# State-space input tables built in matmul layout from a repeated power table, in a hybrid S5 and Fourier inference step

## The chip, the cores and the metric

The kernel runs on one core of a Trainium2 chip. The metric is device time in microseconds (us) for one execution of the whole program; less is better. Engines are named as in the profile: PE (matmul), PEld (its weight load), DVE (vector), ACT (scalar), POOL (GpSimd) and SP, which only issues transfers.

## The reference, cut to what matters

One layer is applied to 1024 latent and 128 context tokens: a normalisation with modulation, a projection `z = h @ w_in`, a state-space branch and a Fourier branch, each gated by a sigmoid, an output projection, and a SwiGLU block. The change lies in the projection's gates and in the state-space branch, which per direction computes

```
step = exp(log_step);  a = exp(lam * step)            # complex, one per group and state
f    = (a - 1) / lam                                  # complex
bu   = u @ (f * b).T                                  # 32 groups, 16 inputs, 64 states
s_t  = a * s_(t-1) + bu_t                             # forward and backward
y    = Re(s @ c.T) + d * u
g_s5, g_f = sigmoid(h @ w_gates)                      # 2 x 1024 columns
```

## The kernel before

The tokens are cut into 144 chunks of T = 8 steps (16 context chunks, 128 latent chunks). The 32 groups are handled in NB = 8 steps of GQ = 4 groups. The 128 partitions of a state tile are 2 directions times 64 states. For one step q the kernel needs three tables:

- `W` [128, 2, 4*128], which takes the state at a chunk's start to its 8 outputs. It is built on DVE from the power table `Aw` and the parameters `Cp` (lines 545 to 550, with `Gt` as scratch).
- `Gt`, the input table: for each group a 128 by 128 matrix from (time in chunk, input) to (direction, state), once real and once imaginary. Its entries are `fA[p, t, g] * b[p, g, h]` as complex numbers, where `fA` is the table of `f * a^t`. DVE builds it with the state on the partitions (lines 552 to 561), PE then transposes each 128 by 128 block (line 566, 8 blocks a step), and ACT copies the result back (line 567), so that it can be a matmul's weights.
- `Tm`, the direct path inside a chunk, built by small matmuls (line 594), stored to DRAM as `kd` and loaded back through a sliding window (line 605).

`fA` and `Aw` are copied by DVE from tables that POOL computes (lines 498 to 501), with the time axis reversed for the backward half.

`s5_run(q)` loads the inputs `U` from DRAM, multiplies them by `Gt` (tile `v`, line 621) and copies the result from PSUM to the state tile `X`: the forward half by ACT (line 625), the backward half with the chunk axis reversed by ACT and DVE (lines 627 to 630). DVE then scans `X` over the chunks (lines 636 to 639). `s5_out(q)` copies `X` to `Xo` on ACT (656 to 658), multiplies by `Tm` and `W` (tile `y`, lines 666 to 668) and stores the outputs.

Between these steps stand nine calls `gate(p)`. Each runs two column blocks of the projection through `in_unit`: the weights `ws` are loaded by SP, split into two parts by ACT (line 93) and DVE (line 94), and 72 matmuls a block (lines 271 to 273) fill three PSUM tiles. The first of them carries two more columns, the shift; DVE copies these to `sh` (line 482), and ACT applies the function with `sh` as bias (lines 483 to 486). The finished pieces `sg` are stored to DRAM as `ind`, issued by SP (line 685).

The program order is

```
pre, run_ = [prep(0)], []
gate(ORD[0])
pre.append(prep(1)); run_.append(s5_run(0, ...))
for q in range(NB):
    run_.append(s5_run(q + 1, ...)); gate(ORD[q]); s5_out(q, ...); pre.append(prep(q + 2))
```

This order is only a priority. A planner orders the instructions of each engine by a simulated timeline, and takes what is ready at its simulated time in this priority; the order on each engine is then fixed, and an engine whose next instruction is not ready waits, with all that stands behind it. Waits between engines are semaphores that the framework sets. Tiles of one tag share `bufs` buffers, and a new tile waits for the readers of the one whose buffer it takes.

Of the kernel before, what the change touches and what calls it, by code (L numbers as in the profile page):

```python
# [22 lines left out]
CH = 384  # L23
# [6 lines left out]
T = 8  # L30
# [31 lines left out]
def tile_flow_step(ctx: ExitStack, tc: tile.TileContext, a, o):  # L62
# [17 lines left out]
    def aux_tile(name):  # L80
        return psp.tile([128, 512], F32, tag="aux", bufs=3, name=name)
# [281 lines left out]
    def st(name, shape, bufs=None):  # L363
        return pS.tile(shape, F32, tag=name, name=name, bufs=bufs)
# [110 lines left out]
    def in_unit(j0, nm, piece, out, func):  # L475
        for f in range(2):
            w = weight(a["w_in"][j0 + f], f"{nm}{f}", eng=V)
            sh = psh.tile([128, 2], F32, tag="sh", bufs=2, name=f"sh{f}_{nm}")
            for t in (2, 0, 1):
                ps, dst = proj_unit(w, t, f"{nm}{f}_{t}"), piece(f, t)  # L480
                if t == 2:
                    V.tensor_copy(sh, ps[:, CH:CH + 2])
                    S.activation(out=dst[:, 0:256], in_=ps[:, 0:256], func=func, bias=sh[:, 0:1])
                    S.activation(out=dst[:, 256:CH], in_=ps[:, 256:CH], func=func, bias=sh[:, 1:2])
                else:
                    S.activation(out=dst, in_=ps[:, 0:CH], func=func, bias=sh[:, 0:1])
                out(f, t, dst)
# [8 lines left out]
    u_unit(1, 1)  # L496
    u_unit(2, 1)
    with tc.issue_after(last[1]):
        for e_, d_, s_ in ((V, fA, Fk), (V, Aw, Ak[:, :, 1:9])):
            e_.tensor_copy(d_[0:64], s_[0:64])  # L500
            e_.tensor_copy(d_[64:128], s_[64:128, :, ::-1])
    pSt.release()
    pwa.release()
    abc = open_pool("abc")
    h_chunk(2)
    u_unit(3, 1)
    u_unit(2, 2)
# [10 lines left out]
    pw.release()  # L518
    pwu.release()
    pa.release()  # L520
    psh = open_pool("psh")
    q5 = open_pool("q5", side="right")

    def s5_prep(q):
        gs = slice(GQ * q, GQ * q + GQ)
        Bp = q5.tile([128, 2, GQ, H], F32, tag="Bp", name=f"Bp{q}")
        SY.dma_start(out=Bp, in_=a["b_p"][:, :, gs, :])
        Cp = q5.tile([128, 2, GQ, H], F32, tag="Cp", name=f"Cp{q}")
        SY.dma_start(out=Cp, in_=a["c_p"][:, :, gs, :])
# [12 lines left out]
        W = q5.tile([128, 2, GQ * 128], F32, tag="W", bufs=NW, name=f"W{q}")
        Gt = q5.tile([128, 2, GQ * 128], F32, tag="G", bufs=NG, name=f"G{q}")
        e_ = V
        V.tensor_tensor(v4(W, 0), bt(Aw, 0), bp(Cp, 0), ALU.mult)
        V.tensor_tensor(v4(Gt, 0), bt(Aw, 1), bp(Cp, 1), ALU.mult)
        V.tensor_tensor(W[:, 0], W[:, 0], Gt[:, 0], ALU.add)
        e_.tensor_tensor(v4(W, 1), bt(Aw, 0), bp(Cp, 1), ALU.mult)
        e_.tensor_tensor(v4(Gt, 1), bt(Aw, 1), bp(Cp, 0), ALU.mult)
        e_.tensor_tensor(W[:, 1], W[:, 1], Gt[:, 1], ALU.subtract)  # L550

        V.tensor_tensor(v4(Gt, 0), bt(fA, 0), bp(Bp, 0), ALU.mult)
        V.tensor_tensor(v4(Gt, 1), bt(fA, 1), bp(Bp, 1), ALU.mult)
        V.tensor_tensor(Gt[:, 0], Gt[:, 0], Gt[:, 1], ALU.subtract)
        V.tensor_tensor(v4(Gt, 1), bt(fA, 0), bp(Bp, 1), ALU.mult)
        gh = GQ // 2
        for hh in range(2):
            gt = q5.tile([128, gh, T, H], F32, tag="gt", name=f"gt{q}{hh}")
            hs, gl = slice(128 * gh * hh, 128 * gh * hh + 128 * gh), slice(gh * hh, gh * hh + gh)
            V.tensor_tensor(gt, bt(fA, 1)[:, gl], bp(Bp, 0)[:, gl], ALU.mult)  # L560
            V.tensor_tensor(Gt[:, 1, hs], Gt[:, 1, hs], gt.rearrange("p g t h -> p (g t h)"), ALU.add)

        for ri in range(2):
            ps = aux_tile(f"gtr{q}_{ri}")
            for g in range(4):
                PE.transpose(ps[:, 128 * g:128 * g + 128], Gt[:, ri, 128 * g:128 * g + 128], ident)
            S.copy(out=Gt[:, ri, :], in_=ps)

        return gs, Bp, Cp, W, Gt

    def s5_prep2(q, gs, Bp, Cp, W, Win):
        bb = q5.tile([128, 3, 2, GQ * H + H], F32, tag="bb", name=f"bb{q}")
        b4 = bb[:, :, :, 0:GQ * H].rearrange("p v r (g h) -> p v r g h", g=GQ)
        bt1 = q5.tile([128, 240], F32, tag="KX", name=f"bt1{q}")[:, 0:2 * GQ * H].rearrange("p (r g h) -> p r g h", r=2, g=GQ)
        shb = [128, GQ, H]
        V.memset(bb, 0.0)
        for ri in range(2):
            fb = [fr2[:, r, gs].unsqueeze(2).to_broadcast(shb) for r in range(2)]
            V.tensor_tensor(b4[:, 0, ri], Bp[:, ri], fb[0], ALU.mult)
            V.tensor_tensor(bt1[:, ri], Bp[:, 1 - ri], fb[1], ALU.mult)  # L580
            V.tensor_tensor(b4[:, 0, ri], b4[:, 0, ri], bt1[:, ri],
                            ALU.subtract if ri == 0 else ALU.add)
        V.tensor_copy(bb[0:64, 1], bb[0:64, 0])
        V.tensor_copy(bb[64:128, 2], bb[64:128, 0])
        KX = q5.tile([128, GQ // 4, 240], F32, tag="KX", name=f"KX{q}")
        for aa in range(GQ // 4):
            ps = aux_tile(f"kx{q}_{aa}")
            for v, cs_ in ((2, slice(0, 112)), (0, slice(112, 128)), (1, slice(128, 240))):
                for ri in range(2):
                    for g4 in range(4):  # L590
                        g = 4 * aa + g4
                        src = (Cp[:, ri, g], W[:, ri, 128 * g:128 * g + 112],
                               W[:, ri, 128 * g + 16:128 * g + 128])[v]
                        PE.matmul(ps[32 * g4:32 * g4 + 32, cs_], bb[:, v, ri, H * g:H * g + 32], src,
                                  start=(ri == 0), stop=(ri == 1), skip_group_check=True)
# [10 lines left out]
        return W, Win, Tm  # L606

    def s5_run(q, Win):
        gs = slice(GQ * q, GQ * q + GQ)
# [5 lines left out]
        n = 0  # L615
        for ri in range(2):
            for g0 in range(0, GQ, 2):
                ng = 2
# [4 lines left out]
                v = ps[:, 0:CC * ng].rearrange("p (g c) -> p g c", g=ng)  # L623
                xg = X[:, ri, g0:g0 + ng]
                S.copy(out=xg[0:64, :, 1:CC + 1], in_=v[0:64])
                if n % 2:
                    V.tensor_copy(xg[64:128, :, CP + 1:CC + 1], v[64:128, :, CC - 1:CP - 1:-1])
                else:
                    S.copy(out=xg[64:128, :, CP + 1:CC + 1], in_=v[64:128, :, CC - 1:CP - 1:-1])
                V.tensor_copy(xg[64:128, :, 1:CP + 1], v[64:128, :, CP - 1::-1])  # L630
                n += 1
        def step(lv, dst, src):
            m = dst.shape[3]
            shp = [128, 2, GQ, m]
# [42 lines left out]
    def gate(p):  # L677
# [1042 lines left out]
def _layout(i):  # L1720
# [72 lines left out]
```

## Time and profile before

| | |
|---|---|
| runs of the kernel before | 1524.16 us median of 3 (1522.48 to 1524.55) |
| the profiled execution's own time | 1526.42 us |
| its span, first to last instruction | 1524.6 us |
| mean granted clock of PE in it | 0.981 |
| PE / DVE / ACT / POOL busy | 1460.6 / 946.5 / 567.1 / 662.1 us |
| moved by DMA | 243.84 MB |

The profiled execution's time lies 1.82 us above its span and 2.26 us above the median of the runs. Times in the trace are counted from the start of the span. The state-space steps and the gates take the stretch from about 98 to 400 us.

### The profile page before, as it was taken

Reading aid. Unit: us, or ns where it says so; the run is one execution under the profiler, and the core shown is the slowest. Engines: PE = TensorE matmul, PEld = TensorE weight load, DVE = VectorE, ACT = ScalarE, POOL = GpSimd, SP = SyncE. Lnnn points to the kernel's source line nnn. Section 1 sums busy time; section 2 is a strip of 40 time slices with the busy share of each in tenths; the row PEclk is TensorE's granted clock in tenths of the full one; section 3 lists DMA queues with packets and bytes.
Section 4 is the critical chain, followed back from the end, with each engine's and each line's share of the span. In section 5 each row is a group of like instructions: output and inputs, shape, how many; then the busy total and the mean of one; then the engine's idle time right before and its main releaser. Section 6 shows DMA issues by size and latency. Waiting matters only on the chain. (4 is left out here: it accounts for less than half of the span.)

```text
span 1524.6 us, 23986 instructions
## 1 busy us (share of the span) xinstructions
PE 1460.6 (96%) x8999; PEld 1312.5 (86%) x8999; DVE 946.5 (62%) x1845; ACT 567.1 (37%) x1096; POOL 662.1 (43%) x599
## 2 busy tenths in 40 slices
PE   6999999999989999999899999999999999999995
PEld 3799998989968779787679999999999998887884
DVE  5557989997245335368964345553345567667788
ACT  7433243343444122355543433433333444112323
POOL 4910000000014111354687778877777972322354
PEclk9999999999989999999999999999999999999998
DMA  9343233232524753354431355444445458667523
GB/s 326 106 126 97 75 109 94 89 106 94 176 76 128 247 169 121 128 206 181 170 127 71 111 197 198 158 177 170 171 183 205 188 194 311 215 219 293 192 69 124
DMA packets 101984, 243.84 MB, mean 160 GB/s; under 512 B 15710, under 2 KB 46047, under 8 KB 101868
## 3 DMA queue, kind: packets, MB, share of 16 engines
q1 hardware_dynamic: 93228, 210.84, 40.0%
q10 hardware_dynamic: 8640, 31.46, 5.2%
q8 instruction: 71, 1.16, 0.3%
q14 instruction: 45, 0.37, 0.1%
HBM read 172.51 MB, written 69.74 MB: 159 GB/s over the span
## 5 line engine op out<-in xcount | busy, mean ns | idle before, releaser
L94 POOL TENSOR_TENSOR wh_glu<-ws_glu,wh_glu 128x512 fp32r<-128x512 f32 x4 | 5.1, 1276 | 338.2 <-DMA St<-in_fS 324.0
L271 PE MATMUL g<-h,wh_g 128*128 128x384 f32 (+1 forms) x432 | 147.5, 341 | 0.0
L272 PE MATMUL g<-h,wh_g 128*128 128x384 f32 (+1 forms) x432 | 147.3, 341 | 0.0
L273 PE MATMUL g<-h,wh_g 128*128 128x384 f32 (+1 forms) x432 | 146.5, 339 | 0.0
L1308 DVE TENSOR_TENSOR stg<-ra,stg 128x512 fp32r<-128x512 f32 x63 | 69.5, 1113 | 71.3 <-ACT stg L1307 71.3
L1416 POOL TENSOR_TENSOR wd<-wd,wd 128x512 f32<-128x512 f32 x25 | 36.5, 1474 | 111.7 <-DMA wd<-in_w_d 48.6
L272 PEld LDWEIGHTS g<-h,wh_g 128*128 128x128 f32 x432 | 81.5, 189 | 0.2 <-issue 0.2
L271 PEld LDWEIGHTS g<-h,wh_g 128*128 128x128 f32 x432 | 81.3, 188 | 0.3 <-issue 0.3
L273 PEld LDWEIGHTS g<-h,wh_g 128*128 128x128 f32 x432 | 81.3, 188 | 0.2 <-issue 0.2
L94 POOL TENSOR_TENSOR wh_pj<-ws_pj,wh_pj 128x512 fp32r<-128x512 f32 x16 | 22.1, 1380 | 104.3 <-ACT wh_pj L93 93.0
L1469 DVE TENSOR_TENSOR acc<-acc,U 128x1024 f32<-128x1024 f32 x34 | 41.4, 1219 | 25.3 <-PE U L1450 25.0
L1307 ACT CAST stg<-ra 128x512 fp32r<-128x512 f32 x63 | 38.5, 617 | 36.4 <-DVE ra L1296 28.4
L963 DVE TENSOR_TENSOR wh_out<-ws_out,wh_out 128x512 fp32r<-128x512 f32 x32 | 34.1, 1081 | 23.5 <-ACT wh_out L962 23.5
L1296 DVE TENSOR_TENSOR ra<-ra 128x512 f32<-128x512 f32 x36 | 46.5, 1292 | 0.3
L1450 PE MATMUL q<-B,A 128*128 128x512 f32 x192 | 45.4, 393 | 0.2 <-DVE tq L1599 0.2
L1450 PEld LDWEIGHTS q<-B,A 128*128 128x128 f32 x192 | 36.0, 188 | 8.8 <-DVE tq L1599 0.6
L923 DVE TENSOR_TENSOR sgc<-sgc,p 128x384 f32<-128x384 f32 x24 | 13.3, 554 | 48.4 <-PE p L106 48.4
L963 POOL TENSOR_TENSOR wh_out<-ws_out,wh_out 128x512 fp32r<-128x512 f32 x16 | 22.0, 1380 | 46.5 <-ACT wh_out L962 44.5
L977 PE MATMUL o<-wh_out,m 128*128 128x512 f32 x96 | 37.1, 414 | 3.5 <-ACT scr0b L1059 3.5
L636 DVE TENSOR_TENSOR ta<-X,Sg 128x56 f32<-128x56 f32 (+10 forms) x88 | 39.0, 443 | 1.1
L639 DVE TENSOR_TENSOR X<-X,tb 128x56 f32<-128x56 f32 (+10 forms) x88 | 39.0, 450 | 0.9
L962 ACT CAST wh_out<-ws_out 128x512 fp32r<-128x512 f32 x48 | 28.2, 616 | 29.2 <-PE o L979 18.9
(1550 smaller groups left out, 4516.8 us busy)
## 6 DMA issues: line engine op xcount, KB each, us to landing
ad<-stg ACTq DMA_DIRECT2D x60, 512.0 KB, 2.9
A<-ad SPq DMA_DIRECT2D x60, 512.0 KB, 6.2
wa<-in_w_ada SPq DMA_DIRECT2D x48, 512.0 KB, 6.1
ws_out<-in_w_out SPq DMA_DIRECT2D x24, 512.0 KB, 3.9
wd<-in_w_d SPq DMA_DIRECT2D x22, 512.0 KB, 9.4
ind<-in SPq DMA_DIRECT2D x54, 192.0 KB, 1.9
ws_g<-in_w_in SPq DMA_DIRECT2D x18, 512.0 KB, 3.5
sgc<-ind SPq DMA_DIRECT2D x48, 192.0 KB, 3.3
```

What stands on the lines that cost most here:

```text
L271: PE.matmul(ps, w[:, 0, wsl], hi, start=first, stop=False)
L272: PE.matmul(ps, w[:, 0, wsl], lo, start=False, stop=False)
L273: PE.matmul(ps, w[:, 1, wsl], hi, start=False, stop=last)
L636: V.tensor_tensor(A, src, Sc[:, 0, lv, gs].unsqueeze(1).unsqueeze(3).to_broadcast(shp), ALU.mult)
L639: V.tensor_tensor(dst, dst, B[:, ::-1], ALU.add)
L963: (eng or PL).tensor_tensor(w[:, 1, :], src, f32(w[:, 0, :]), ALU.subtract)
L977: PE.matmul(p, mc[t][0][:, k, ts_], w[n][:, 0], start=(k == 0), stop=False)
L1296: V.tensor_tensor(a_[out], a_[x], a_[y], op)
L1307: S.copy(out=st_[:, 0], in_=src)
L1308: V.tensor_tensor(st_[:, 1], src, f32(st_[:, 0]), ALU.subtract)
L1450: PE.matmul(ps, A[:, va], B[:, vb], start=(first and ti == 0 and i == 0), stop=(last and ti == n - 1 and i == 2), skip_group_check=True)
L1469: V.tensor_tensor(dst, dst, ps, ALU.add)
```

## The change

`Gt` is no longer built with the state on the partitions and transposed. Instead `fA` itself is transposed once, in four 128 by 128 blocks, written to a DRAM table `fad` as three parts (real, minus imaginary, imaginary), and in each step a load repeats each row of that table over 16 partitions (`FA_`), so that it lies as (time, input) on the partitions and (group, state) in the free axis. The parameters `b` come in a second layout `b_t`, made on the host, and a load repeats them over the 8 times (`Bt`). Three DVE operations of 128 by 1024 elements then give `Gt` as the matmul wants it. They stand at the end of `s5_prep2`. The scratch for `W` becomes a tile of its own, `Wt`.

The loads of a step (`Bp`, `Cp`, `FA_`, `Bt`) are issued at the start of the step before, in two buffers each. The stores of the gates' pieces are issued by ACT in place of SP. The copy of the shift columns and the copies of the backward half of the state go from DVE to ACT.

```diff
-    fA = st("fA", [128, 2, T, G])
+    fA = st("fA", [128, 2, NB, T, GQ])
...
-                    V.tensor_copy(sh, ps[:, CH:CH + 2])
+                    S.copy(out=sh, in_=ps[:, CH:CH + 2])
...
-        for e_, d_, s_ in ((V, fA, Fk), (V, Aw, Ak[:, :, 1:9])):
-            e_.tensor_copy(d_[0:64], s_[0:64])
-            e_.tensor_copy(d_[64:128], s_[64:128, :, ::-1])
+        V.tensor_copy(Aw[0:64], Ak[0:64, :, 1:9])
+        V.tensor_copy(Aw[64:128], Ak[64:128, :, 8:0:-1])
+        for ri in range(2):
+            for rows, ts in ((slice(0, 64), slice(None)), (slice(64, 128), slice(None, None, -1))):
+                V.tensor_copy(fA[rows, ri], Fk[rows, ri, ts].rearrange("p t (q g) -> p q t g", g=GQ))
...
+    ft = psh.tile([128, 6, 128], F32, tag="ft", name="ft")
+    fad = dram.tile([NB * T, 3, GQ, 128], F32, tag="fad", name="fad")
+    ps_ = aux_tile("fat")
+    for b in range(4):
+        PE.transpose(ps_[:, 128 * b:128 * b + 128], fA[:, b // 2, 4 * (b % 2):4 * (b % 2) + 4], ident)
+    S.copy(out=ft[:, 0:2], in_=ps_[:, 0:256])
+    S.activation(out=ft[:, 2:4], in_=ps_[:, 256:512], func=AF.Copy, scale=-1.0)
+    S.copy(out=ft[:, 4:6], in_=ps_[:, 256:512])
+    for b in range(2):
+        for z in range(3):
+            SY.dma_start(out=fad[32 * b:32 * b + 32, z], in_=ft[:, 2 * z + b])
...
+    def s5_load(q):
+        gs = slice(GQ * q, GQ * q + GQ)
+        Bp = q5.tile([128, 2, GQ, H], F32, tag="Bp", bufs=2, name=f"Bp{q}")
+        SY.dma_start(out=Bp, in_=a["b_p"][:, :, gs, :])
+        Cp = q5.tile([128, 2, GQ, H], F32, tag="Cp", bufs=2, name=f"Cp{q}")
+        SY.dma_start(out=Cp, in_=a["c_p"][:, :, gs, :])
+        FA_ = q5.tile([128, 3, GQ * 128], F32, tag="FA", bufs=2, name=f"FA{q}")
+        n3, n2 = 3 * GQ * 128, 2 * GQ * 128
+        SY.dma_start(out=FA_, in_=bass.AP(tensor=fad.tensor, offset=fad.offset + T * n3 * q,
+                                          ap=[[n3, T], [0, H], [1, n3]]))
+        Bt = q5.tile([128, 2, GQ * 128], F32, tag="Bt", bufs=2, name=f"Bt{q}")
+        b_t = a["b_t"]
+        SY.dma_start(out=Bt, in_=bass.AP(tensor=b_t.tensor, offset=b_t.offset + n2 * q,
+                                         ap=[[0, T], [NB * n2, H], [1, n2]]))
+        tabs[q] = (Bp, Cp, FA_, Bt)
...
     def s5_prep(q):
-        Bp = ...; SY.dma_start(...); Cp = ...; SY.dma_start(...)
+        if q + 1 < NB:
+            s5_load(q + 1)
+        Bp, Cp, FA_, Bt = tabs.pop(q)
...
-        V.tensor_tensor(v4(Gt, 0), bt(fA, 0), bp(Bp, 0), ALU.mult)
-        V.tensor_tensor(v4(Gt, 1), bt(fA, 1), bp(Bp, 1), ALU.mult)
-        V.tensor_tensor(Gt[:, 0], Gt[:, 0], Gt[:, 1], ALU.subtract)
-        V.tensor_tensor(v4(Gt, 1), bt(fA, 0), bp(Bp, 1), ALU.mult)
-        for hh in range(2):
-            V.tensor_tensor(gt, bt(fA, 1)[:, gl], bp(Bp, 0)[:, gl], ALU.mult)
-            V.tensor_tensor(Gt[:, 1, hs], Gt[:, 1, hs], gt.rearrange("p g t h -> p (g t h)"), ALU.add)
         for ri in range(2):
-            ps = aux_tile(f"gtr{q}_{ri}")
-            for g in range(4):
-                PE.transpose(ps[:, 128 * g:128 * g + 128], Gt[:, ri, 128 * g:128 * g + 128], ident)
-            S.copy(out=Gt[:, ri, :], in_=ps)
+            V.tensor_tensor(v4(W, ri), bt(Aw, 0), bp(Cp, ri), ALU.mult)
+            V.tensor_tensor(v4(Wt, ri), bt(Aw, 1), bp(Cp, 1 - ri), ALU.mult)
+            V.tensor_tensor(W[:, ri], W[:, ri], Wt[:, ri], ALU.subtract if ri else ALU.add)
...
+        V.tensor_tensor(Gt, FA_[:, 0:1].to_broadcast([128, 2, GQ * 128]), Bt, ALU.mult)
+        V.tensor_tensor(FA_[:, 1:3], FA_[:, 1:3], Bt[:, ::-1], ALU.mult)
+        V.tensor_tensor(Gt, Gt, FA_[:, 1:3], ALU.add)
...
                 S.copy(out=xg[0:64, :, 1:CC + 1], in_=v[0:64])
-                if n % 2:
-                    V.tensor_copy(xg[64:128, :, CP + 1:CC + 1], v[64:128, :, CC - 1:CP - 1:-1])
-                else:
-                    S.copy(out=xg[64:128, :, CP + 1:CC + 1], in_=v[64:128, :, CC - 1:CP - 1:-1])
-                V.tensor_copy(xg[64:128, :, 1:CP + 1], v[64:128, :, CP - 1::-1])
+                S.copy(out=xg[64:128, :, CP + 1:CC + 1], in_=v[64:128, :, CC - 1:CP - 1:-1])
+                S.copy(out=xg[64:128, :, 1:CP + 1], in_=v[64:128, :, CP - 1::-1])
...
-        in_unit(j0, f"g{p}", piece, lambda f, t, t_: SY.dma_start(out=dst[f][:, CH * t:CH * t + CH], in_=t_), fu)
+        in_unit(j0, f"g{p}", piece, lambda f, t, t_: S.dma_start(out=dst[f][:, CH * t:CH * t + CH], in_=t_), fu)
...
+    s5_load(0)
     pre, run_ = [prep(0)], []
```

## Rows read from the trace of the kernel before

**Rows 1.** The page's first part: busy time, share of the span, instructions.

```profile
PE 1460.6 (96%) x8999; PEld 1312.5 (86%) x8999; DVE 946.5 (62%) x1845; ACT 567.1 (37%) x1096; POOL 662.1 (43%) x599
```

**Rows 2.** Stretches of 100 to 400 us: each engine's busy us, clock, DMA share.

```profile
140.00:360.00 220.00, 210.27 (x1529) 204.09 (x1528) 208.37 (x574) 83.22 (x170) 0.00 (x0) 0.99 0.29 93
...
sum 300.00, PE 290.27 PEld 282.59 DVE 249.43 ACT 109.36 POOL 0.00; mean PE 96.76 PEld 94.20 DVE 83.14 ACT 36.45 POOL 0.00
```

**Rows 3.** Waits of PE, 100 to 400 us: us in total, times, longest.

```profile
PE y L667 <- ACT Xo L658: 5.4, 4, 2.1
PE v L621 <- DMA U<-ud: 3.1, 2, 2.4
PE v L621 <- DVE X L630: 0.8, 1, 0.8
```

**Rows 4.** Stretches of 2 us after a stall of PE, columns as in rows 2.

```profile
188.00:190.00 2.00, 2.00 (x11) 2.00 (x10) 1.81 (x4) 0.63 (x2) 0.00 (x0) 0.50 0.30 102
190.00:192.00 2.00, 2.00 (x13) 2.00 (x13) 0.00 (x1) 0.40 (x2) 0.00 (x0) 0.71 0.02 5
```

**Rows 5.** Timeline of PE around four transposes: start us, us, instruction.

```profile
114.63 0.34 PE L273 MATMUL g<-h,wh_g 128*128 128x386 f32 x1
114.81 0.34 PE L271 MATMUL g<-h,wh_g 128*128 128x386 f32 x1
114.99 0.60 PE L566 MATMUL gtr<-ident,G 128*128 128x128 f32 x4
...
115.61 0.34 PE L273 MATMUL g<-h,wh_g 128*128 128x386 f32 x1
```

**Rows 6.** The transposes as a group, 100 to 400 us: busy us, mean ns.

```profile
L566 PE MATMUL gtr<-ident,G 128*128 128x128 f32 x64 | 10.4, 275 | 0.4 <-DVE G L554 0.4
```

**Rows 7.** DVE groups, 100 to 400 us: busy us, mean ns, idle before.

```profile
L627 DVE COPY X<-v 64x256 f32<-64x256 f32 x16 | 6.8, 427 | 2.4 <-ACT X L625 1.9
L560 DVE TENSOR_TENSOR gt<-fA,Bp 128x256 f32<-128x256 f32 x16 | 6.8, 425 | 6.8 <-DMA Bp<-in_b_p 6.7
...
L630 DVE COPY X<-v 64x32 f32<-64x32 f32 x32 | 6.0, 190 | 1.2 <-ACT X L629 0.7
L554 DVE TENSOR_TENSOR G<-G 128x512 f32<-128x512 f32 x8 | 5.5, 690 | 0.2
...
L482 DVE COPY sh_g<-g 128x2 f32<-128x2 f32 x18 | 2.8, 156 | 6.0 <-PE g L273 5.7
```

**Rows 8.** Readers of tile g5s: duration ns min/median/max.

```profile
L1550 DVE TENSOR_TENSOR acc<-acc,g5s x8: 1218/1226/2307, 1439.9 to 1497.2; 128x1024 f32<-128x1024 f32 x8
```

**Rows 9.** ACT groups, 100 to 400 us, columns as in rows 7.

```profile
L567 ACT COPY G<-gtr 128x512 f32<-128x512 f32 x16 | 9.4, 587 | 14.9 <-PE gtr L566 14.3 <-DVE tb L637 0.6
...
L629 ACT COPY X<-v 64x256 f32<-64x256 f32 x16 | 5.9, 370 | 0.2
...
L657 ACT COPY Xo<-X 64x128 f32<-64x128 f32 x8 | 2.4, 297 | 0.1
```

**Rows 10.** ACT groups, 59 to 70 us: a small copy.

```profile
L175 ACT COPY mod<-pm 128x8 f32<-128x8 f32 x2 | 0.3, 165 | 0.9 <-PE pm L168 0.9
```

**Rows 11.** Transfers issued by ACT's queue: ns min/median/max.

```profile
L1310 ACTq DMA_DIRECT2D ad<-stg x60: 326/326/359, 873.0 to 1237.9; - x60
```

**Rows 12.** Half-us stretches with the load of T, then ws_g; last columns: DMA share, GB/s.

```profile
218.50:219.00 0.50, 0.50 (x5) 0.50 (x4) 0.50 (x4) 0.00 (x0) 0.00 (x0) 1.00 0.61 166
220.50:221.00 0.50, 0.50 (x5) 0.50 (x4) 0.50 (x4) 0.00 (x0) 0.00 (x0) 1.00 0.87 344
```

**Rows 13.** Timeline of SP, 95 to 107 us.

```profile
103.53 0.38 SPq L99 DMA_DIRECT2D ws_g<-in_w_in  x1
```

**Rows 14.** Timeline of PE: the first matmul of the second gate.

```profile
126.28 0.34 PE L271 MATMUL g<-h,wh_g 128*128 128x386 f32 x1
```

**Rows 15.** PE groups, 68 to 100 us (three lines of this kind).

```profile
L271 PE MATMUL u<-h,wh_us 128*128 128x384 f32 x24 | 8.1, 338 | 0.0
```

**Rows 16.** Timeline of DVE, 70 to 73 us.

```profile
72.07 0.44 DVE L501 COPY fA<-Fk 64x512 f32<-64x512 f32 x1
```

More of the change, by code (lines that the diff above doesn't have):

```diff
@@ L504, in tile_flow_step @@
     abc = open_pool("abc")
+    psh = open_pool("psh")
+    ft = psh.tile([128, 6, 128], F32, tag="ft", name="ft")
[9 more added lines that the diff above has]
+            SY.dma_start(out=fad[32 * b:32 * b + 32, z], in_=ft[:, 2 * z + b])
     h_chunk(2)
@@ L520, in tile_flow_step @@
     pa.release()
-    psh = open_pool("psh")
     q5 = open_pool("q5", side="right")
+    tabs = {}
+    def s5_load(q):
[13 more added lines that the diff above has]
+        tabs[q] = (Bp, Cp, FA_, Bt)
     def s5_prep(q):
         gs = slice(GQ * q, GQ * q + GQ)
[L526 to L529, printed above, removed]
+        if q + 1 < NB:
+            s5_load(q + 1)
+        Bp, Cp, FA_, Bt = tabs.pop(q)
         V.tensor_scalar(Cp[:, 1], Cp[:, 1], -1.0, None, ALU.mult)
@@ L543, in s5_prep, with s5_prep2 @@
         Gt = q5.tile([128, 2, GQ * 128], F32, tag="G", bufs=NG, name=f"G{q}")
[L544 to L550, printed above, removed]
-        V.tensor_tensor(v4(Gt, 0), bt(fA, 0), bp(Bp, 0), ALU.mult)
-        V.tensor_tensor(v4(Gt, 1), bt(fA, 1), bp(Bp, 1), ALU.mult)
-        V.tensor_tensor(Gt[:, 0], Gt[:, 0], Gt[:, 1], ALU.subtract)
-        V.tensor_tensor(v4(Gt, 1), bt(fA, 0), bp(Bp, 1), ALU.mult)
-        gh = GQ // 2
-        for hh in range(2):
-            gt = q5.tile([128, gh, T, H], F32, tag="gt", name=f"gt{q}{hh}")
-            hs, gl = slice(128 * gh * hh, 128 * gh * hh + 128 * gh), slice(gh * hh, gh * hh + gh)
-            V.tensor_tensor(gt, bt(fA, 1)[:, gl], bp(Bp, 0)[:, gl], ALU.mult)
-            V.tensor_tensor(Gt[:, 1, hs], Gt[:, 1, hs], gt.rearrange("p g t h -> p (g t h)"), ALU.add)
-        for ri in range(2):
-            ps = aux_tile(f"gtr{q}_{ri}")
-            for g in range(4):
-                PE.transpose(ps[:, 128 * g:128 * g + 128], Gt[:, ri, 128 * g:128 * g + 128], ident)
-            S.copy(out=Gt[:, ri, :], in_=ps)
-        return gs, Bp, Cp, W, Gt
-    def s5_prep2(q, gs, Bp, Cp, W, Win):
+        Wt = q5.tile([128, 2, GQ * 128], F32, tag="Wt", name=f"Wt{q}")
+        for ri in range(2):
+            V.tensor_tensor(v4(W, ri), bt(Aw, 0), bp(Cp, ri), ALU.mult)
+            V.tensor_tensor(v4(Wt, ri), bt(Aw, 1), bp(Cp, 1 - ri), ALU.mult)
+            V.tensor_tensor(W[:, ri], W[:, ri], Wt[:, ri], ALU.subtract if ri else ALU.add)
+        return gs, Bp, Cp, W, Gt, FA_, Bt
+    def s5_prep2(q, gs, Bp, Cp, W, Gt, FA_, Bt):
         bb = q5.tile([128, 3, 2, GQ * H + H], F32, tag="bb", name=f"bb{q}")
@@ L605, in s5_prep2 @@
         SY.dma_start(out=Tm, in_=win)
-        return W, Win, Tm
+        V.tensor_tensor(Gt, FA_[:, 0:1].to_broadcast([128, 2, GQ * 128]), Bt, ALU.mult)
+        V.tensor_tensor(FA_[:, 1:3], FA_[:, 1:3], Bt[:, ::-1], ALU.mult)
+        V.tensor_tensor(Gt, Gt, FA_[:, 1:3], ALU.add)
+        return W, Gt, Tm
     def s5_run(q, Win):
@@ L614, in s5_run @@
         V.memset(X[:, :, :, 0:1], 0.0)
-        n = 0
         for ri in range(2):
@@ L625, in s5_run @@
                 S.copy(out=xg[0:64, :, 1:CC + 1], in_=v[0:64])
-                if n % 2:
-                    V.tensor_copy(xg[64:128, :, CP + 1:CC + 1], v[64:128, :, CC - 1:CP - 1:-1])
-                else:
-                    S.copy(out=xg[64:128, :, CP + 1:CC + 1], in_=v[64:128, :, CC - 1:CP - 1:-1])
-                V.tensor_copy(xg[64:128, :, 1:CP + 1], v[64:128, :, CP - 1::-1])
-                n += 1
+                S.copy(out=xg[64:128, :, CP + 1:CC + 1], in_=v[64:128, :, CC - 1:CP - 1:-1])
+                S.copy(out=xg[64:128, :, 1:CP + 1], in_=v[64:128, :, CP - 1::-1])
         def step(lv, dst, src):
@@ L1768, in _layout @@
         r[n + "_p"] = np.stack([v.reshape(128, G, H) for v in ri], 1)
+    r["b_t"] = r["b_p"].reshape(128, 2, NB, GQ, H).transpose(4, 2, 1, 3, 0)
     r["h0"] = i["state_s5"][0, 0].transpose(0, 3, 1, 2).reshape(128, 2, G)
```

## Prediction

> **What bounds the kernel now.** I read the busy times first, and there PE has 1460.6 of 1524.6 us [rows 1]: nothing else can set the length of the whole, and a change pays only through PE's own work, its stalls or its clock. The chain that ended last is no help here, since it reaches back only over the last stages, far behind the change. So I read next the stretch that the change touches, the state-space steps and gates from 100 to 400 us. There PE is busy 290.27 of 300 us. Between 140 and 360 us DVE is nearly as full, 208.37 of 220 beside PE's 210.27, while ACT has 83 and POOL nothing [rows 2]. The reader is to see two engines close to their limit, of which PE is the one that sets the length. Before 140 and after 360 us it has no gap; it loses 9.7 us (300 less 290.27), all between 140 and 360. The waits say to whom: 5.4 us to the copies `Xo`, which wait for DVE's scan, 3.1 us to the load of `U`, 0.8 us to DVE's copies of `X` [rows 3], and 0.4 us to the transposes' source [rows 6]. After the first long stall PE's granted clock falls to its lower level, 1.2 of 2.4 GHz, and is 0.50 and 0.71 over the next two stretches of 2 us [rows 4]: lost are 2*(1-0.50) + 2*(1-0.71) = 1.6 us.
>
> So the stage's length is PE's work, plus 9.7 us of stalls, plus 1.6 us of slow clock. Each part of the change is worth what it does to these three.
>
> **The transposes.** Four of them stand between two gate matmuls. From one matmul to the next PE takes 0.18 us (114.63 to 114.81); from 114.81 to 115.61 it starts two matmuls and four transposes, so four transposes cost 0.80 - 0.36 = 0.44 us, 0.11 each [rows 5]. The 64 that go are worth 7.0 us, and the four new ones on `fA` cost 0.44: 6.6 us come off. The other bound is their mean duration, 275 ns [rows 6]: 60 * 0.275 = 16.5 us. I take 6.6, because on this engine a new instruction starts before the last one has ended, and the distance of starts is what the gates see.
>
> **DVE.** For `Gt` it loses four operations of 128 by 512 a step, 5.5 us a line over the 8 steps, and four of 128 by 256 (two products, two sums of the same size), 6.8 us a line: 22.0 + 13.6 us. The copies of `X` that go to ACT are 6.8 + 6.0 us, the shift copies 2.8 us [rows 7]. Together 51.2 us. It gains 24 operations of 128 by 1024. The nearest row is a product of that shape with one repeated operand, 1.226 us [rows 8]; the other bound is twice a 128 by 512, 1.38 us [rows 7]. That is 29.4 to 33.1 us; I take 29.4. DVE becomes 21.8 us lighter, and its wait of 6.7 us for `Bp` [rows 7] goes, since `Bp` is loaded a step earlier. `W` has the same six operations as before. DVE isn't the bound, so this counts only as far as PE waits for DVE: the 5.4 and 0.8 us of rows 3. A tenth less work in a stretch that is 95% full lets each scan end some 3.6 us (28.5/8) sooner a step, more than the longest of those waits, 2.1 us. But the planner makes a new order from its own estimate of a lighter DVE and will set `y` earlier too. I take half, 3.1 us, with 0 and 6.2 as bounds. The 0.4 us goes with the transposes. If the longest stall goes, so does the slow clock behind it: 1.6 us.
>
> **ACT.** It loses 16 copies, 9.4 us. It gains 16 copies of 64 by 256 at 0.370 us, 5.9 us [rows 9]; 32 of 64 by 32, for which the bounds are 0.165 [rows 10] and 0.297 us [rows 9], and at 0.2 they are 6.4 us; 18 shift copies at 0.165, 3.0 us; and 54 transfers to issue at 0.326 us [rows 11], 17.6 us. That is 23.5 us more on 109.4 [rows 2], 133 of about 290 us, so it is hidden by ACT's idle time. Queued behind these on ACT are `Xo` and the gates' pieces, and PE waits for both; with no cover the price would be 23.5/8 = 2.9 us a step. SP is rid of 54 issues and of standing before pieces that ACT hasn't finished. I count nothing for that, since no wait of PE but that for `U` goes back to SP.
>
> **The new loads.** A step loads 768 KB of `FA_` and 512 KB of `Bt`, 1.31 MB. Both repeat an outer dimension of 8, and the trace has one load of that form, the window load of `T`: while it runs alone the DMA share is 0.61 and the rate 166 GB/s, against 0.87 and 344 GB/s for the weights that follow it [rows 12]. By the first rate the pair takes 7.9 us a step, by the second 3.8 us. I take 7.9. It is issued a step ahead of its use, and a step is about 36 us (290/8), so for itself it is hidden; what counts is what stands behind it in SP's queue. At the start these are the loads for steps 0 and 1, 15.8 us, and then the weights of the second gate, issued at 103.53 [rows 13]. These would land near 119; their first matmul is at 126.28 [rows 14], so some 7 us of cover are left. Later weights have such cover too. `U` has none: it has two buffers, its load waits until `y` of two steps before is done, and PE already waits for it [rows 3]. I leave the 3.1 us as they are; the bounds are 0, if SP's freer queue issues `U` at once, and the rival below.
>
> By the Trainium skill, "DMA: Bandwidth & Descriptors", rules for kernel authors, the outermost dimension that isn't 1 sets how many of the 16 engines a transfer uses, so a leading dimension of 8 confines it to 8. The rates of rows 12 agree with that. By a spread over all 16 the pair would take the 3.8 us, and the rival below would be worth half.
>
> **The way of `fA`.** Its copies end at 72.5 us now [rows 16]. Four copies of 64 by 256, at most 0.427 us each [rows 7], take 1.7 in place of 0.95 us, so it is whole near 73.3. The four transposes wait for that, and on PE everything queued behind them would. PE has 72 projection matmuls of 384 columns after 68 us [rows 15], 72 * 0.18 = 13 us, most of which stand before the transposes in program order; so I count nothing. If the planner sets the transposes first, PE stands from 68 to 73.3, 5.3 us. ACT's three copies and SP's six stores follow at about 80 us, and the table is needed by the loads after 100 us.
>
> **Sum.** 6.6 + 3.1 + 0.4 + 1.6 = 11.7 us off the profiled execution's 1526.42: 1514.7. That execution lies 2.26 us above the median of the runs, so the forecast is 1512.5 us.
>
> **Rivals.** *Only the transposes.* The stalls aren't a want of DVE but a mismatch between the planner's times and the chip's, and form again elsewhere: 1524.2 - 6.6 = 1517.6. For it: the stalls are few and scattered, at most 2.4 us each [rows 3]. Against: two thirds of them end on DVE, at its fullest.
>
> *All stalls go.* 6.6 + 9.7 + 1.6 = 17.9 us: 1506.3. For it: DVE gets slack and SP's queue frees `U`. Against: `U` depends on `y`, not on DVE. With the upper price of the transposes in the forecast's sum the time is 1524.2 - (16.5 + 5.1) = 1502.6; I use this only as the low end.
>
> *`U` behind the bulk loads: slower.* If `FA_` and `Bt` of a later step are issued just before `U`, `v` waits up to 7.9 us. Steps 2 to 7 can be hit. One and a half of them (11.7/7.9) eat the gain; three give 1512.5 + 23.7 = 1536. For it: `U` is already late. Against: buffers of `FA_` come free when `Gt` of the step is done, while `U` waits for `y`, so they fall together only by chance, some 8 of 36 us.
>
> *The change shifts a stall instead of removing one: the same.* PE waits for `fA` for 5.3 us and only the transposes come off: 1524.2 - 6.6 + 5.3 = 1522.9. For it: POOL ends late, and DVE waits for its tables. Against: the work that stands before it in program order.
>
> **How the numbers follow.** The forecast has 0.5 (its own range, with 0 to 6.2 us for the stalls on DVE, 1509 to 1516), only the transposes 0.2, all stalls 0.1, slower 0.1, the same 0.1. Less than 0.2%, 3 us, can't be told from no change. Faster are the first three, 0.8; within 0.2% 0.1; slower 0.1. The range holds the first three and leaves out the last two: from 1502.5, the upper price of the transposes, to 1521, the edge of no change.
>
> **What would show it.** In the profile after: no `gtr` and four transposes near 77 to 81 us without a wait of PE; PE's idle time from 100 to 400 us near 6 us; DVE near 228 us and ACT near 133 us busy there; the last gate matmul some 12 us earlier, and the stages behind it unchanged in length. `FA_` and `Bt` together should take near 8 us. Wrong would be: PE waits for `U`, `FA_` or weights of several us a step; PE waits for pieces that ACT hasn't copied out; a stall at 68 to 74 us; or an end of the gates that is earlier but given back behind 400 us.

## Result and the profile after

The changed kernel takes 1549.51 us (median of 4 runs, 1543.89 to 1553.12), the kernel before 1523.32 in runs beside it; the ratio is 1.0164, with a 95% interval of 1.0142 to 1.0187. It is slower by some 26 us, where 12 us faster was forecast, and it lies outside the range. The profiled execution of after spans 1550.8 us, 26.2 more than that of before.

Where the time goes is a question of one stage. The first matmul of the last gate (`uf`) starts at 395.77 us before and at 419.13 after, so 23.4 of these are lost by there. The stretches of after, columns as in [rows 2], say in which part:

```profile
100.00:200.00 100.00, 83.14 (x603) 81.63 (x603) 64.44 (x164) 27.48 (x70) 0.00 (x0) 0.91 0.56 169
200.00:300.00 100.00, 80.56 (x547) 78.59 (x547) 72.47 (x174) 36.55 (x85) 0.00 (x0) 0.91 0.43 117
300.00:400.00 100.00, 99.59 (x738) 97.98 (x737) 88.58 (x232) 41.81 (x104) 0.00 (x0) 1.00 0.32 100
...
140.00:160.00 20.00, 6.11 (x71) 5.78 (x72) 8.68 (x23) 4.39 (x13) 0.00 (x0) 0.57 0.50 152
```

PE is idle for 36.7 us of the 300, against 9.7 before [rows 2], and all but 0.4 of that before 300 us. From the first gate matmul to that of `uf`, before and after:

```profile
98.56:395.77 297.21, 287.48 (x2065) 279.80 (x2065) 249.49 (x681) 110.20 (x223) 0.00 (x0) 0.99 0.31 100
100.01:419.13 319.12, 282.41 (x2001) 277.32 (x2001) 230.14 (x575) 114.02 (x273) 0.00 (x0) 0.95 0.42 126
```

27.0 us more idle, less 5.1 us of PE's busy time, and a start 1.45 us later make the 23.4. The 64 transposes that are gone (2065 against 2001 matmuls) should have taken more off the busy time; the slower clock, 0.95 instead of 0.99 on the mean, makes what is left take longer. In the worst 20 us PE works for 6.11. What is more telling: DVE is busy for 230.1 us instead of 249.5, 19.4 less where 21.8 was forecast, and still PE waits for its results. These are PE's waits in after from 60 to 430 us, as in [rows 3]:

```profile
PE kx L606 <- DVE bb L596: 20.6, 2, 16.9
PE y L678 <- ACT Xo L669: 14.5, 3, 7.3
PE v L636 <- DMA U<-ud: 1.6, 1, 1.6
```

and these are DVE's, 100 to 430 us, of which before has only one for `Bp`, at another place [rows 7]:

```profile
DVE FA L619 <- DMA FA<-fad: 27.9, 6, 8.0
...
DVE G L618 <- DMA Bt<-in_b_t: 9.8, 2, 6.6
...
DVE bb L591 <- DMA Bp<-in_b_p: 4.9, 1, 4.9
```

The reader is to put the two together: DVE stands for 37.7 us before the new products, because their operands haven't landed, and PE stands for 35.1 us (`kx` and `y`) before what comes behind the products in DVE's order: `bb`, and the scan, from which ACT copies `Xo`. The timeline of DVE shows one such place (start us, us, instruction, idle before it and its releaser):

```profile
129.80 1.23 DVE L618 TENSOR_TENSOR G<-FA,Bt 128x1024 f32<-128x1024 f32 x1 [3.25 <-DMA Bt<-in_b_t]
...
139.13 0.68 DVE L94 TENSOR_TENSOR wh_g<-ws_g,wh_g 128x512 fp32r<-128x512 f32 x1
142.03 1.23 DVE L619 TENSOR_TENSOR FA<-FA,Bt 128x1024 f32<-128x1024 f32 x1 [2.22 <-DMA FA<-fad]
...
145.25 0.35 DVE L593 TENSOR_TENSOR bb<-bb,bt 128x64 f32<-128x64 f32 x2
152.21 1.23 DVE L619 TENSOR_TENSOR FA<-FA,Bt 128x1024 f32<-128x1024 f32 x1 [6.60 <-DMA FA<-fad]
153.35 0.23 DVE L595 COPY bb<-bb 64x160 f32<-64x160 f32 x1
153.59 0.24 DVE L596 COPY bb<-bb 64x160 f32<-64x160 f32 x1
```

The two products at L619 belong to steps 2 and 3, the copies of `bb` behind them to step 1. The planner's order has work of later steps there, before the `bb` of step 1; on the chip DVE stands 6.60 us for a load of step 3, and `bb`, for which PE already waits, comes after it. PE's timeline has the other side of it, a stand of 16.86 us (from 137.03) at `kx` of step 1:

```profile
153.89 0.97 PE L606 MATMUL kx<-W,bb 128*32 128x112 f32 x16 [16.86 <-DVE bb L596]
```

SP's timeline has the loads themselves:

```profile
104.46 0.68 SPq L548 DMA_DIRECT2D FA<-fad  x1
105.20 0.62 SPq L552 DMA_DIRECT2D Bt<-in_b_t  x1
...
107.80 0.62 SPq L552 DMA_DIRECT2D Bt<-in_b_t  x1
...
129.77 0.60 SPq L548 DMA_DIRECT2D FA<-fad  x1
135.65 0.62 SPq L552 DMA_DIRECT2D Bt<-in_b_t  x1
142.00 0.58 SPq L548 DMA_DIRECT2D FA<-fad  x1
```

The `FA_` issued at 142.00 is there at 152.21, 10.2 us later, that of 129.77 at 142.03, 12.3 us later.

ACT stands as well. Its rows below are the last part of a gate's piece, that piece's store, and behind it the next piece:

```profile
120.90 0.36 ACT L484 ACTIVATE in<-g,sh_g 128x128 f32<-128x128 f32 x1
130.07 0.33 ACTq L696 DMA_DIRECT2D ind<-in  x1
130.44 0.58 ACT L486 ACTIVATE in<-g,sh_g 128x384 f32<-128x384 f32 x1 [9.18 <-DMA Bp<-in_b_p]
```

The piece is done at 121.26 and its store issued 8.8 us later; the profile names `Bp`, a load that SP issued at 115.74, as what ended the wait. In the order built for ACT that store waits for the piece and for one of the semaphores that count transfers (the listing has eight, which SP's transfers use too):

```
L696 DMA ind_1280<-in_2_1410 128x384 [waits DMAHW5_49,Activation_49]
```

The count that it waits for on `DMAHW5` is the one that the load of `Bp` for step 2 completes, so the order and the profile name the same load. So a store on ACT's queue can stand until a load of SP's has landed. ACT's waits for transfers add up to 30.1 us in the stage (9.2 + 6.2 + 4.9 + 4.6 + 3.7 + 1.5).

The theories to be told apart: **T1**, the repeated loads are slow, land late, and DVE, working in a fixed order, hands the delay on. **T2**, ACT standing at the gate stores is the loss. **T3**, the copies moved to ACT lengthen the way from `v` to the scan and to `Xo`. Beside these, that the planner merely built a worse order.

### The profile page after: what moved, and what is told of

Its sections match the earlier page's. It is cut to its first block, busy times and chain, and to the rows that moved or that the text cites. A ratio compares the mean times of both kernels' runs of the same rounds, so it can differ in the third digit from the quotient of the medians.

```text
span 1550.8 us, 23818 instructions
## 1 busy us (share of the span) xinstructions
PE 1457.6 (94%) x8939; PEld 1311.5 (85%) x8939; DVE 925.6 (60%) x1739; ACT 571.9 (37%) x1151; POOL 665.3 (43%) x599
## 5 line engine op out<-in xcount | busy, mean ns | idle before, releaser
L1481 DVE TENSOR_TENSOR acc<-acc,U 128x1024 f32<-128x1024 f32 x34 | 41.4, 1218 | 25.3 <-PE U L1462 25.0
L647 DVE TENSOR_TENSOR ta<-X,Sg 128x576 f32<-128x576 f32 (+10 forms) x88 | 38.9, 443 | 5.8 <-ACT X L642 4.9
L486 ACT ACTIVATE in<-g,sh_g 128x384 f32<-128x384 f32 x36 | 21.0, 582 | 51.5 <-PE g L273 37.0
```

The source lines that it names most:

```text
L647: V.tensor_tensor(A, src, Sc[:, 0, lv, gs].unsqueeze(1).unsqueeze(3).to_broadcast(shp), ALU.mult)
L1481: V.tensor_tensor(dst, dst, ps, ALU.add)
```

## Experiments

Each ratio is to runs of the kernel before on the same chip, with its 95% interval. The expectations call DVE VectorE, ACT ScalarE and SP SyncE.

**The loads spread over more rows (e1).** In the changed kernel both loads have 8 outer rows. Here the table is stored twice, so that its load has 16, and the host lays the parameters out with their repeats, so that theirs has 128.

```diff
-    fad = dram.tile([NB * T, 3, GQ, 128], F32, tag="fad", name="fad")
+    fad = dram.tile([NB * T, 2, 3, GQ, 128], F32, tag="fad", name="fad")
...
-            SY.dma_start(out=fad[32 * b:32 * b + 32, z], in_=ft[:, 2 * z + b])
+            for c in range(2):
+                SY.dma_start(out=fad[32 * b:32 * b + 32, c, z], in_=ft[:, 2 * z + b])
...
-        SY.dma_start(out=FA_, in_=bass.AP(tensor=fad.tensor, offset=fad.offset + T * n3 * q,
-                                          ap=[[n3, T], [0, H], [1, n3]]))
+        SY.dma_start(out=FA_, in_=bass.AP(tensor=fad.tensor, offset=fad.offset + 2 * T * n3 * q,
+                                          ap=[[n3, 2 * T], [0, H // 2], [1, n3]]))
...
-                                         ap=[[0, T], [NB * n2, H], [1, n2]]))
+                                         ap=[[NB * n2, 128], [1, n2]]))
```

> The changed kernel, but the repeated loads have 16 or 128 outer rows instead of 8: the power table is written twice to DRAM, so that its load has rows of (step, copy), 16 of them, and the input table is laid out with its repeats, so that its load has 128 rows. Bytes, instructions and issuing engine stay. T1 (the loads use half of the transfer engines and land late; VectorE stands on them 27.9 + 9.8 us in the stage and the scan and the kx inputs behind it): VectorE's waits for FA and Bt fall from 37.7 us to under 12, PE's waits for bb and Xo from 35.1 to under 15, and the time to 1525 to 1535. T2 (ScalarE stands at its issues of the gate stores): some of that wait goes too, since it waits for the same slow loads, but 1540 or more. T3 (copies on ScalarE lengthen the chain): 1545 to 1550, unchanged. By the Trainium skill, DMA: Bandwidth & Descriptors, the load should then run on all 16 engines, in about half the time.

Measured: 1511.85 us, ratio 0.9919 (0.9896 to 0.9942): not only is the loss gone, the forecast gain is there, and the time is below what each of the three theories had said. The stretches of the changed kernel while the loads of the first steps run, columns as in [rows 2] (DMA share and GB/s are the last two),

```profile
107.00:113.00 6.00, 6.00 (x37) 6.00 (x36) 5.69 (x16) 1.43 (x3) 0.00 (x0) 1.00 0.65 162
113.00:119.00 6.00, 6.00 (x77) 5.57 (x76) 0.00 (x0) 0.86 (x2) 0.00 (x0) 1.00 0.59 177
```

and the same of this run:

```profile
107.00:113.00 6.00, 6.00 (x37) 6.00 (x36) 5.43 (x16) 1.74 (x4) 0.00 (x0) 1.00 1.03 264
113.00:119.00 6.00, 6.00 (x77) 5.57 (x76) 5.42 (x8) 1.81 (x6) 0.00 (x0) 1.00 1.03 298
```

The same bytes go at 264 to 298 GB/s instead of 162 to 177, with all transfer engines busy instead of some 0.6 of them, and DVE has 5.42 us of work from 113 to 119 us where it had none. Its waits and PE's (100 to 430 and 60 to 430 us):

```profile
DVE FA L620 <- DMA FA<-fad: 6.3, 6, 2.5
...
PE y L679 <- ACT Xo L670: 5.4, 3, 3.0
...
PE v L637 <- DMA U<-ud: 1.9, 1, 1.9
PE kx L607 <- DVE bb L597: 0.6, 1, 0.6
```

This run also settles the planner. Of the 1739 instructions of DVE's built order one copy of `bb` stands further on than in the changed kernel, ACT's order is the same, and on PE three instructions have moved. So nearly the same order was built for loads of 8 rows and of 16 and 128, and what changed is the chip's time for it. What the stage lost it lost to the loads. By the Trainium skill, "DMA: Bandwidth & Descriptors", rules for kernel authors, an outermost dimension of 8 confines a transfer to at most 8 engines, and one of a multiple of 16 is how to use all 16; the shares of 0.6 and 1.03 agree.

**The gate stores back on SP (e2).**

```diff
-        in_unit(j0, f"g{p}", piece, lambda f, t, t_: S.dma_start(out=dst[f][:, CH * t:CH * t + CH], in_=t_), fu)
+        in_unit(j0, f"g{p}", piece, lambda f, t, t_: SY.dma_start(out=dst[f][:, CH * t:CH * t + CH], in_=t_), fu)
```

> The changed kernel with the gate stores issued from SyncE again; the rest is as changed. T1 (slow loads on VectorE's path): VectorE's waits for FA and Bt stay near 35 us, and the time is 1543 to 1550. T2 (ScalarE's own queue stands at the issues): ScalarE's some 30 us of waits for transfers go, PE's waits for Xo go with them, and the time is 1525 to 1537. T3: no change, 1545 to 1550.

Measured: 1542.64 us, ratio 1.0112 (1.0086 to 1.0139) beside the changed kernel's 1.0164: some 8 us better (0.0052 * 1524), the least that the intervals can tell. DVE's waits for FA and Bt are 31.1 us, PE's for `bb` 18.0 and for `Xo` 13.4. ACT goes on standing, now for the buffers of pieces whose store SP issues late:

```profile
ACT in L486 <- DMA ind<-in: 17.5, 2, 8.8
...
ACT KX L608 <- DMA ind<-in: 12.6, 1, 12.6
```

These waits add up to 30.1 us, as long as ACT's in after, so this run prices who issues the stores, some 8 us, and not ACT's standing as such.

**The copies back on DVE (e3).** The shift copy and the state copies as the diff of the change shows them on its minus side; stores and loads as changed.

> The changed kernel with the shift columns and the state copies back on VectorE, as they were before; the rest is as changed. T1: VectorE gets some 15 us more work and the loads stay late: 1548 to 1556. T2: the same, ScalarE still stands at its issues: 1545 to 1553. T3 (the three copies in a row on ScalarE delay the scan and so Xo and y): PE's wait for Xo falls from 14.5 us to near 5, and the time to 1535 to 1541.

Measured: 1562.27 us, ratio 1.0244 (1.0205 to 1.0282), worse, and by more than T1 had said. T3 falls: moving the copies to ACT softened the loss. One row stands out, ACT's wait for shift columns, which DVE, itself standing before `FA_` for 36.4 us, hands out late:

```profile
ACT in L483 <- DVE sh_g L482: 95.4, 14, 14.5
```

That it is the reason isn't shown: the kernel before has such a wait too (29.2 us by that name), and with mended loads one as long costs 0.3% (e11).

**The moves to ACT alone (e4).** The kernel before with the gate stores, shift columns and state copies of the change, and its own tables, transposes and loads.

> The kernel before with only the moves to ScalarE: gate stores, shift columns and state copies; tables, transposes and loads as before. T1 (all of the loss is in the table's loads): 1518 to 1526, no loss. T2 (issuing stores from ScalarE makes it stand, whatever the loads): ScalarE waits for transfers for 15 us or more in the stage, and the time is 1532 to 1545. T3 (the copies): PE waits for Xo for over 10 us, 1530 to 1538.

Measured: 1522.21 us, ratio 0.9981 (0.9969 to 0.9994). ACT waits 3.5 us for a transfer that isn't its own weight, where after has 30.1, although it issues the same 54 stores. So on the old tables, without the slow loads, issuing from ACT costs nothing, and the moves are worth 0.2%.

**The loads as they are, but the products later (e5).** The three products of a step are held behind `bb` of the same step.

```diff
-        V.tensor_copy(bb[64:128, 2], bb[64:128, 0])
+        ib = V.tensor_copy(bb[64:128, 2], bb[64:128, 0]).ins
...
+        with tc.issue_after(ib):
+            V.tensor_tensor(Gt, FA_[:, 0:1].to_broadcast([128, 2, GQ * 128]), Bt, ALU.mult)
+            V.tensor_tensor(FA_[:, 1:3], FA_[:, 1:3], Bt[:, ::-1], ALU.mult)
+            V.tensor_tensor(Gt, Gt, FA_[:, 1:3], ALU.add)
```

> The changed kernel with its slow loads as they are; the three products with the power table are held behind the operands bb of their own step in VectorE's order, where the changed kernel has products of steps 2 and 3 ahead of the bb of step 1. Bytes, rows and issuing engines stay. T1 as I now put it (a late load costs what stands behind it in VectorE's order: bb, kx and with them the kernel's window load T): PE's wait for bb falls from 20.6 us to under 6, Xo's 14.5 us may stay, and the time is 1526 to 1537. Rival T1b (the loads' rate is the whole cause, whatever the order; the wait only moves to the products and from there to v and Xo): PE's waits add up to 30 us or more all the same, 1543 to 1552.

Measured: 1541.7 us, ratio 1.0128 (1.0101 to 1.0154). Neither theory's numbers fit: PE's wait for `bb` falls to 12.6 us, not under 6, and its three waits sum to 28.0 us (with 11.9 for `Xo` and 3.5 for a weight). The rows of DVE say why:

```profile
DVE Cp L561 <- DMA Cp<-in_c_p: 19.1, 4, 7.2
DVE bt L592 <- DMA kd<-KX: 11.8, 3, 6.3
...
DVE G L619 <- DMA Bt<-in_b_t: 5.7, 1, 5.7
```

DVE no longer waits for `FA_` at all. It waits for `Cp`, 64 KB, whose load is issued amid the bulk loads, and for the store of `kd` before a buffer of `KX` comes free. Beside the slow loads a small transfer is late as well: `Cp` issued at 126.20 was there at 136.28, 10.1 us later, where an `FA_` of the changed kernel took 10.2 and 12.3. So the order of DVE mostly decides which of them it stands at. What the order by itself is worth, some 5 us, is near what the intervals can tell.

**One load at a time (e6).** Only the table `fad` is stored twice; `Bt` keeps its 8 rows.

> The changed kernel with the power table alone written twice, so that its load has 16 outer rows; the input table keeps its 8. T1, if each load counts by its own wait on VectorE (27.9 us for the power table, 9.8 for the input table): three quarters of the way from the changed kernel to the run with both loads changed, 1518 to 1525. If the two loads share the same 8 transfer engines and the slower of the pair sets the time: less than half the way, 1530 to 1545. T2: 1540 or more.

Measured: 1529.72 us, ratio 1.0043 (1.002 to 1.0067); its ten runs go from 1526.59 to 1540.66, and the profiled one is the longest, so its rows aren't used. From 1.0164 to 0.9919 this is half the way, 0.0121 of 0.0245: between the two expectations. 768 of 1,280 KB a step are mended, and half of the loss is.

**Both loads mended, the stores on SP (e7).** The edits of the first two experiments together.

> Both repeated loads with 16 or 128 outer rows, and the gate stores issued from SyncE as in the kernel before. If stores on ScalarE cost only because they stood behind slow loads (the changed kernel gained 0.4% from moving them back): no difference to the first run, 1509 to 1515. If they cost by themselves: 1503 to 1508. If they are a gain by themselves, as the kernel before with the moves alone (0.998) leaves open: 1515 to 1520.

Measured: 1510.63 us, ratio 0.9919 (0.9903 to 0.9935). The same as the first run: with loads that land in time it doesn't matter who issues the gate stores.

**Both loads mended, the products later (e8).** The edits of the first experiment and of the fifth.

> Both repeated loads with 16 or 128 outer rows, and the products held behind bb of their own step as in e5_order. T1: with loads that land in time the order costs nothing and nothing is left to gain but the 0.6 us for bb: 1508 to 1514. Rival T1b: the same. If the order by itself is worth something (PE's waits for Xo, 5.4 us): 1503 to 1508.

Measured: 1515.84 us (1510.55 to 1519.79), ratio 0.9945 (0.9929 to 0.9962). Holding the products back gains nothing and may cost a little; the median lies just above the range expected, 1508 to 1514. The profiled execution is the shortest of the nine, so its rows (PE waits 9.2 us for `Xo` instead of 5.4, DVE 6.7 us for `Cp`) don't explain that.

**Without most of the loads (e9).** From step 2 on no `FA_` and `Bt` are loaded; the products read what the loads of steps 0 and 1 left in the buffers, so the kernel leaves out the right tables of six steps.

```diff
+        if q > 1:
+            tabs[q] = (Bp, Cp) + keep[q % 2]
+            return
...
-        tabs[q] = (Bp, Cp, FA_, Bt)
+        keep[q] = (FA_, Bt)
+        tabs[q] = (Bp, Cp) + keep[q]
```

> The changed kernel, 8 outer rows, without the loads of the power and input tables from step 2 on: the products of steps 2 to 7 take what stands in the two pairs of buffers, so their state-space tables are wrong and the transfers of 6 of the 8 steps are left out. All work of the engines stays. T1 (the transfers' own time): VectorE's waits for FA go but for those of steps 0 and 1, ScalarE's waits behind them and PE's waits for bb and Xo fall to under 12 us, 1509 to 1522. Rival (what costs is the work that the change puts on VectorE and ScalarE and its order, not the transfers): 1535 or more.

Measured: 1516.99 us, ratio 0.9946 (0.9919 to 0.9973). All of DVE's and ACT's work is there, and two thirds of the gain too. DVE's only waits for the bulk loads are those for `Bt` of steps 0 and 1, still from 8 rows, and PE's for `bb` and `Xo` are 8.3 us instead of 35.1:

```profile
DVE G L622 <- DMA Bt<-in_b_t: 9.2, 2, 5.2
...
PE kx L610 <- DVE bb L600: 6.6, 1, 6.6
...
PE y L682 <- ACT Xo L673: 1.7, 3, 0.6
```

This is the second, independent sign that the loads' time is the loss.

**The new tables alone, loads mended (e10).** No move to ACT: stores, shift columns and state copies as before.

> The changed tables with 16 or 128 outer rows, without any of the moves to ScalarE: gate stores on SyncE, shift columns and state copies as in the kernel before. If the parts add up, with 0.2% (2.9 us) for the moves by the run of the kernel before with them alone: about 1515, 1512 to 1518. If VectorE needs the moves to keep up with the new products: 1519 or more. If the whole gain is the table's (transposes and VectorE's lighter work): 1508 to 1512.

Measured: 1527.37 us, ratio 1.0015 (0.9998 to 1.0031). This I hadn't expected: the parts don't add up. The moves alone are worth 0.2%, the tables alone nothing, both together 0.8%. PE is busy for 280.3 us to the first matmul of `uf`, 7.2 less than before, but idle for 18.3 instead of 9.7: what the transposes gave, stalls took. The waits in this run, of PE, of DVE and of ACT:

```profile
PE y L684 <- ACT Xo L675: 7.7, 4, 3.8
PE v L638 <- DMA U<-ud: 7.2, 3, 3.6
...
DVE X L647 <- ACT X L646: 12.7, 4, 5.4
...
ACT in L483 <- DVE sh_g L482: 55.7, 11, 9.2
```

Two more runs start from e7 and split the copies: e11 has the shift columns back on DVE, e12 the state copies.

> The run e7 (loads with 16 or 128 outer rows, gate stores on SyncE, 1510.6 us) with the shift columns alone back on VectorE; the state copies stay on ScalarE. In e10, with both back, ScalarE waited 55.7 us for shift columns and VectorE 12.7 us for ScalarE's state copies, 1527.4 us. If the shift column makes the loss (ScalarE stands at a column that VectorE has queued behind products and scans, and the state copies behind that): 1520 to 1528, ScalarE's wait for shift columns over 40 us and PE's waits over 12 us. If the state copies make it: 1509 to 1514.

Measured: 1518.82 us, ratio 0.9949 (0.9933 to 0.9965), between the two ranges. PE's wait for `Xo` is 8.0 us. The profile gives ACT's wait for shift columns as 21.8 us, but there is more of it under another name. "issue" is a wait for which the profile shows no cause:

```profile
ACT in L483 <- issue: 71.3, 10, 12.0
```

Each of these ten ends within 0.1 us of the end of DVE's copy of the columns, as here:

```profile
136.82 0.15 DVE L482 COPY sh_g<-g 128x2 f32<-128x2 f32 x1
...
137.06 0.47 ACT L483 ACTIVATE in<-g,sh_g 128x256 f32<-128x256 f32 x1 [9.44 <-issue]
```

So ACT stands for the columns for some 93 us, about as long as in e3, and the kernel loses 0.3% by it. (In e10 it is 84.8 us, 55.7 and 29.1 of "issue" that end in the same way.)

> The run e7 with the state copies alone back on VectorE and ScalarE in turn, as in the kernel before; the shift columns stay on ScalarE. If the split of the state copies over two engines makes the loss of e10: 1520 to 1528, VectorE's wait for ScalarE's copies stays near 12 us. If the shift column makes it: 1509 to 1515, and that wait falls under 5 us. If it takes both: 1512 to 1519 here and in e11.

Measured: 1525.6 us, ratio 0.9994 (0.9973 to 1.0015); DVE's wait for ACT's copies is 11.0 us, as expected if the split state copies make the loss; PE's for `U` is 6.2 and for `Xo` 6.9. So of the 0.96% between e7 and e10 the state copies make 0.75% (0.9994 - 0.9919) and the shift columns 0.3% (0.9949 - 0.9919). A timeline of e10 shows one place where that lies (SP's issue, then PE and the copies):

```profile
197.84 0.50 SPq L629 DMA_DIRECT2D U<-ud  x1
...
204.63 1.74 PE L638 MATMUL v<-U,G 128*128 128x144 f32 x12 [1.49 <-DMA U<-ud]
205.42 0.39 ACT L642 COPY X<-v 64x288 f32<-64x288 f32 x1 [2.19 <-PE v L638]
...
206.23 0.20 DVE L647 COPY X<-v 64x32 f32<-64x32 f32 x1 [5.08 <-ACT X L646]
```

`U` waits for `y` of two steps before, lands 6.8 us after its issue, and PE, ACT and DVE stand one behind another for it. In e7 PE doesn't wait for `U`. Why `y` and so `U` come later when DVE makes some of the state copies was not separated from the order that the planner builds for it, which differs.

## Why the prediction was wrong

**The step that failed** is in the part on the new loads: "It is issued a step ahead of its use, and a step is about 36 us (290/8), so for itself it is hidden". It wasn't: DVE stood for 37.7 us before the new products. With the same bytes in loads of 16 and 128 rows (e1) that is 6.9 us, and the loss is gone.

The rate was right: 166 GB/s was read from the load of `T` [rows 12], 162 GB/s ran. The time of a load was not: a single `FA_`, beside other transfers, took 10.2 and 12.3 us where 7.9 was put for the pair, and the two pairs at the start, put at 15.8 us, were all in use only 25.3 us after the first bulk issue (104.46 to 129.80; `U` and other transfers shared the time).

And the cover was wrong. A step ahead in program order isn't a step ahead in time: the built order has products of steps 2 and 3 before `bb` of step 1, and DVE stood there. With the loads mended, nearly the same order costs nothing (e1); with most of them gone neither (e9). By itself the order is the smaller part: with the products held back (e5) DVE stands for `Cp`, `kd` and `Bp` instead, and some 5 us come back. The prediction named the right form and the rule that speaks against it, and then weighed it only for `U`.

**The rival for the other side** had the right culprit, the bulk loads, at the wrong place. PE waits for `U` for 1.6 us in after, less than before; the damage came by DVE's waits, for the loads themselves or for `Cp`, `Bp` and `kd` that are issued amid them (e5). Its 1536 was an undercount, since only `U` was counted as queued behind.

**ACT's part**, "so it is hidden by ACT's idle time", held for the work and for the issues (e4, e7), but not for a wait that the count of busy time can't show: an issue that stands for someone else's transfer. Taking the issues off ACT gave back some 8 us while the loads were slow (e2), and nothing once they weren't (e7).

**What was right** shows in e1, and luck has a part in it. The forecast's sum was -11.7 us; 0.9919 is -12.4 (1525.83 * 0.0081). The first matmul of `uf` starts at 384.01, 11.8 us earlier than before, where 12 had been said. But the terms are others:

```profile
99.70:384.01 284.31, 276.37 (x2001) 271.48 (x2001) 229.57 (x575) 114.08 (x273) 0.00 (x0) 1.00 0.48 141
```

PE's idle time is 7.9 us instead of 9.7, so stalls gave 1.8 where 3.5 was counted. The clock is 1.00, so its 1.6 us came. PE's busy time fell by 11.1 us (287.48 - 276.37); without the clock's 1.6 that leaves 9.5 for the 64 transposes, the only matmuls that went, where 7.0 had been read from one place [rows 5]. These 12.9 us, less a start 1.1 us later, are the 11.8: one term too large and one too small, which happen to cancel. The products took 1.22 us each, as the nearest row [rows 8] had it. The way of `fA` cost PE no wait.

**By its own terms wrong even there**: the transposes' 6.6 us were to come off whatever else happens, DVE's lighter load was given 3.1 us by itself, and the moves to ACT nothing. The runs show them bound together: tables alone 1.0015 (e10), moves alone 0.9981 (e4), both 0.9919 (e7). For the tables alone the rivals' doubt was right: the stalls formed again elsewhere, and took even what the transposes gave.

**Left open**: how the 26 us divide between DVE's stand and ACT's, since no run kept the one and took away the other; and why the state copies on DVE cost 0.75% with the new tables.

## What to carry to other kernels

A load that repeats rows is priced by its outer rows: write the source twice, or lay it out with its repeats, before judging the change that needs it. The same bytes in 16 and 128 rows instead of 8 turned 1.6% slower into 0.8% faster here. And a prefetch hides a transfer only if every engine that works in a fixed order has something else to do until it lands; ask where the planner will put the first reader, what stands behind that reader, and who waits for it. Where a change has several parts, run them apart and together: here the parts' gains didn't add.

## What the hardware showed beside that

Engines that issue transfers can stand for a transfer of another queue: ACT's gate store at 130.07 came 8.8 us after its piece, when the load of `Bp` that the profile names had landed, and within 0.3 us of DVE's first use of the `Bt` that landed late (129.80 us). That the shared semaphore is the cause is read from the built order, where the count that the store waits for is the one that this load completes; it was not tried with more semaphores. And 64 KB of `Cp` took 10.1 us beside the bulk loads, as long as 768 KB of `FA_`; DVE stood for it for up to 7.2 us (e5).
